# Moving x operands into attention's last slots, down's first steps, and an earlier normed split, in a hybrid encoder step

## The chip, the cores and the metric

The kernel runs on one core of a Trainium2 chip. A core has five engines that run their own instruction queues in order: TensorE (PE, matmuls; its weight loads are shown apart as PEld), VectorE (DVE), ScalarE (ACT), GpSimd (POOL) and SyncE (SP, which here only issues DMA transfers). The engines wait for each other through semaphores. The metric is the device time of one execution in microseconds; less is better.

## The reference

One layer of a streaming encoder is applied to 1024 prompt frames and 32 sample frames of width 1024, all in float32:

```python
h = rms_norm(x, g_mix)
z = h @ w_in                       # q | k | v | conv_h | conv_B | conv_C | gate_a | gate_b
a = window_attn(q, k, v, sink) @ w_attn_out
bo = (cb * causal_conv3(cc * ch)) @ w_conv_out
x = x + (sigmoid(ga) * a + sigmoid(gb) * bo) @ w_mix_out
x = x + mem_attn(rms_norm(x, g_cross) @ w_cq) @ w_co
x = x + square(relu(rms_norm(x, g_mlp) @ w_up)) @ w_down
y = rms_norm(x, g_final)
```

Attention is banded (window 128, chunks of 64 frames, 16 query heads on 4 key heads, a sink in the denominator). K, V, conv states and the memory's keys and values are outputs too.

## The kernel before

**Tiles.** Frames lie along the free dimension in three chunks: 0 and 1 with 384 columns, 2 with 288 (256 prompt and 32 sample frames). The width 1024 lies in 8 blocks f of 128 partitions. Every float32 product is made of three matmuls: an operand is split into a rounded part hi (ACT, L120) and a rest lo (DVE, L121), and `gemm` adds hi·hi, hi·lo and lo·hi (L176 to L178). So each weight tile of 512 KB is loaded by SP (`wr`), split into `wh` and `wl`, and used for 24 matmuls per chunk. `fetch_w`, `issue_w` and `next_w` keep weights up to LOOK = 2 ahead.

**Products in pairs.** For most of the input projection, for up and for down, the chunks 0 and 1 are handled by a scheme of 2x2 block products with fewer multiplications. It needs sums of operands and of weights. For the input projection the operands are, for k = 0 to 3, T2, N1, N3 and N4, made by `x_kind(k)` from the raw inputs: four loads (L801), two multiplications by the norm gain on ACT (L803, L804), one subtraction and three fused multiply-subtracts on DVE (L806 to L810), four hi casts on ACT (L817) and four lo subtractions on DVE and POOL (L819, L821). N4 goes to buffers of the old X1 operands. The weights of a pair come by `pair_fetch` (L829, L830); `pair_issue(key, 4)` first adds them on POOL (L839 to L842) into single buffers s31 and s24 and then splits the sum. `product` runs 12 matmuls (L857 to L859). `x_start` runs the first products of pairs 0 and 1 early; `x_p1` copies a first product out of its bank on ACT (L900) before `x_p2` adds to the same bank. `x_pair` does the rest of a pair; its callbacks ("B11", "W1", "W4", "W3", "W2") fetch and split the next pair's weights.

**Attention's slots.** Attention runs beside the input projection. `hosts` lists 16 column tiles, each with three chunks, so there are 48 slots. For each key head, units of scores, turn (transposes) and values are put at slots by `at`; the fourth head's last unit has its values at slot 45. `sum_step` and `sum_done` add weights of down on POOL in the same slots. At slot 46 `s_begin` calls `open_s`, which closes attention's pool and the kv pool, opens the pools for the pairs in their place, and calls `x_kind(0)` and `x_kind(1)`. The last single column tile, ("b", 1), runs its chunks in the order 1, 0, 2 and carries `x_kind(2)`, `x_kind(3)` and the first pair weights as extras.

**Mix and cross-attention.** `trunk(c)` is a list of 8 items `do_conv_out` and 8 items `do_mix` of chunk c. `beside` puts the steps of cross-attention of the chunk before (`cross_steps`) and late extras between these items. `do_mix` adds to x on DVE (L1101). `do_co` (L1240 to L1242) is cross-attention's output projection; it reads what `Cross.values` split (L1221 to L1227) and its sums are added by DVE (L1245). `normed(c, at)` puts `normed_split(c, f)` behind item at + f: a DVE multiply (L1268), a store, an ACT cast (L1271) and a DVE subtract (L1272), the two DVE operations pinned to program order. It is called with 6 for chunk 0, beside `trunk(2)`.

**Down.** `open_down` opens new pools; PSUM gets six banks `acc` and two `pt`. `steps` is the list (0,0), (0,1), (1,0), (1,1), ... of (j, t): column group j, half t of the hidden blocks k (t = 0: k = 0 to 7, t = 1: k = 8 to 15). `beside_two` runs for each step 24 matmuls of `prod` (chunks 0 and 1) and 24 of `two` (chunk 2), both by `part` (L1654 to L1656), and loads and splits coming operands by `pump`. For the first kind, b11, the blocks k = 0 to 7 lie in Y buffers and 8 to 15 in M buffers; the hidden blocks of chunk 2 lie in Y and H buffers.

**The order of the work.** The program is written down in full and a planner then orders each engine's instructions by dependencies, by program order as priority and by its own simulation of time; instructions given to `pin` keep their order on their engine. A pool opened with `reuse_waits="tile"` lets a new tile wait only for those old tiles whose memory it covers.

Of the kernel before, what the change touches and what calls it, by code (L numbers as in the profile page):

```python
# [38 lines left out]
def hybrid_step(ctx: ExitStack, tc: tile.TileContext, io):  # L39
# [377 lines left out]
    def open_att():  # L417
        closed(st_cm)
        A["cm"], A["pool"] = opened("att", bufs=1, reuse_waits="tile", side="right")
        C["pool"], C["bufs"] = A["pool"], 1  # L420
        C["cvt"] = A["pool"].tile([P, 4, 4], F32, name="cvt")
        W["pool"] = A["pool"]
        do_KS(0)
        do_KS_rest(0)
# [291 lines left out]
    def at(slot, fn):  # L716
        events.setdefault(slot, []).append(fn)
# [30 lines left out]
    for kv, starts in enumerate([(0, 1, 2, 4, 5, 6, 8, 9, 10)] * 3 + [(0, 1, 2, 3, 4, 5, 6, 7, 8)]):  # L748
# [11 lines left out]
        for k in ((5, 8, 11), (2, 5, 8, 11), (2, 5, 8, 11), (2, 5))[kv]:  # L760
            at(base + k, sum_step)
    at(44, sum_done)
    at(46, lambda: s_begin())
    for i, h in enumerate(h for stage in hosts for h in stage):
# [14 lines left out]
    def open_s():  # L779
        closed(A["cm"])  # L780
        closed(kv_cm)
        S["tk_cm"], S["tk"] = opened("tk", bufs=1, reuse_waits="tile")
        S["pw_cm"], S["pw"] = opened("pw", bufs=1, reuse_waits="tile")
        S["cv_cm"], C["pool"] = opened("cv", bufs=1, reuse_waits="tile", side="right")
        C["bufs"] = 2
        C["cvt"] = C["pool"].tile([P, 4, 4], F32, name="cvt")
        S["xk_cm"], S["xk"] = opened("xk", bufs=1, reuse_waits="tile", side="right")
        PW["pool"] = S["pw"]

    PW = {}  # L790
# [5 lines left out]

    def x_kind(k):

        b12, b22, b11, b21 = (S["xk"].tile([P, 384], F32, tag="xk", bufs=8, name=nm("xk")) for _ in range(4))
        for t, c, f in ((b12, 1, k), (b22, 1, k + 4), (b11, 0, k), (b21, 0, k + 4)):  # L800
            sp.dma_start(t, io[f"x{c}"][:, f])  # L801
        g, g4 = col(G_MIX + k), col(G_MIX + k + 4)
        act.mul(b12, b12, g)  # L803
        act.mul(b22, b22, g4)  # L804
        n3 = b22
        dve.tensor_sub(n3, b12, b22)  # L806
        n1, t2, n4 = b12, b11, b21
        dve.scalar_tensor_tensor(n1, b11, g, b12, op0=ALU.mult, op1=ALU.subtract)
        dve.scalar_tensor_tensor(t2, b11, g, n3, op0=ALU.mult, op1=ALU.subtract)
        dve.scalar_tensor_tensor(n4, b21, g4, t2, op0=ALU.mult, op1=ALU.subtract)  # L810
        for kind, x in (("T2", t2), ("N1", n1), ("N3", n3), ("N4", n4)):
            if kind == "N4":
                hi, lo = slot(xpool, "X1", 384), slot(xpool, "X1", 384)
            else:
                hi, lo = (S["tk"].tile([P, 384], F32R, tag="tk", bufs=24, name=nm("tk")) for _ in range(2))
            xk[kind, k] = hi, lo
            act.copy(hi, x)  # L817
            if kind in ("T2", "N1"):
                dve.tensor_sub(lo, x, hi.bitcast(F32))  # L819
            else:  # L820
                pool_e.tensor_tensor(lo, x, hi.bitcast(F32), op=ALU.subtract)  # L821


    raws, wset = {}, {}
# [8 lines left out]
    def pair_issue(key, which):  # L833
        r1, r2 = raws[key][:2]
        a, b = slice(0, 512), slice(512, 1024)
        if which == 4:
            s31 = PW["pool"].tile([P, 1024], F32, tag="s31", name=nm("s31"))
            s24 = PW["pool"].tile([P, 1024], F32, tag="s24", name=nm("s24"))
            pool_e.tensor_tensor(s31[:, b], r2[:, a], r2[:, b], op=ALU.add)  # L839
            pool_e.tensor_tensor(s24[:, a], r1[:, a], s31[:, b], op=ALU.add)  # L840
            pool_e.tensor_tensor(s24[:, b], r1[:, b], s24[:, a], op=ALU.add)
            pool_e.tensor_tensor(s31[:, a], r1[:, a], r2[:, a], op=ALU.add)  # L842
            raws[key] += [s31, s24]
        src = {1: 0, 2: 1, 3: 2, 4: 3}[which]
# [4 lines left out]
        split(hi, lo, raws[key][src])  # L849
        wset[key, which] = (hi, lo)  # L850

    def product(acc, w, half, acts, start):
# [128 lines left out]

    def s_begin():
        open_s()
        for k in range(2):
            x_kind(k)

    ex = [(1, lambda: x_kind(2)), (0, lambda: [x_kind(3), x_fetch(0), x_issue(0, 1), x_fetch(1)]),
          (2, lambda: [x_issue(0, 2), x_issue(1, 1)])]
# [450 lines left out]
    def open_down():  # L1439
# [5 lines left out]
        n_acc = 6  # L1445
        ps.tile([P, 384], F32, tag="pt", bufs=2, name=nm("pt"))

# [98 lines left out]
    normed = lambda c, at: [(at + f, lambda f=f: normed_split(c, f)) for f in range(NF)]  # L1546
    left = beside(left + cross_steps(1), trunk(2), normed(0, 6))
    left = beside(left + cross_steps(2), up0(0) + up0(1), [(min(f + 1, NF - 1), x) for f, x in normed(1, 0)])
# [179 lines left out]

    def beside_two(w, kind, then, half, f, begin, more=(), each=None):

# [14 lines left out]
    def alone(w, kind, then, begin=True, end=True, more=None):  # L1745
        for j, t in steps:
# [6 lines left out]
            if more and (j, t) == (1, 0):  # L1753
# [3 lines left out]
    beside_two(0, "b11", ((*C12, True, False), (*C21, False, False), (*C22, False, False), (*C11, True, False)), 0, 0, True,  # L1757
               twos(1, 0), lambda n: n > 3 and refold(n - 4))
    want(twos(1, 1), ops("n4")[4:], ops("n4")[:4])
# [130 lines left out]
```

## Time and profile before

| what | us |
|---|---|
| three runs | 1788.21, 1789.87, 1792.88 |
| median | 1789.87 |
| the profiled execution, its own time | 1794.17 |
| its span, first to last instruction | 1792.4 |
| PE busy | 1743.3 (97%) |
| DVE busy | 1217.7 (68%) |
| ACT busy | 846.9 (47%) |
| POOL busy | 714.6 (40%) |

The span is what the profiler's rows cover; 1.8 us of the execution lie around it. A row of windows gives a stretch, its length, then for each engine its busy time and the number of instructions, then the granted clock of PE (1.00 is full), the busy share of the DMA engines and their rate. A row of waits names who waited, for which instruction, and the total, the number and the longest of these waits. A row of the timeline gives start, duration, engine, line, operation, output and inputs, and in brackets the idle time before and what ended it.

### The profile page before, as it was taken

Reading aid. Unit: us, or ns where it says so; the run is one execution under the profiler, and the core shown is the slowest. Engines: PE = TensorE matmul, PEld = TensorE weight load, DVE = VectorE, ACT = ScalarE, POOL = GpSimd, SP = SyncE. Lnnn points to the kernel's source line nnn. Section 1 sums busy time; section 2 is a strip of 40 time slices with the busy share of each in tenths; the row PEclk is TensorE's granted clock in tenths of the full one; section 3 lists DMA queues with packets and bytes.
Section 4 is the critical chain, followed back from the end, with each engine's and each line's share of the span. In section 5 each row is a group of like instructions: output and inputs, shape, how many; then the busy total and the mean of one; then the engine's idle time right before and its main releaser. Section 6 shows DMA issues by size and latency. Waiting matters only on the chain.

```text
span 1792.4 us, 30083 instructions
## 1 busy us (share of the span) xinstructions
PE 1743.3 (97%) x11006; PEld 1717.7 (96%) x11006; DVE 1217.7 (68%) x2096; ACT 846.9 (47%) x1624; POOL 714.6 (40%) x749
## 2 busy tenths in 40 slices
PE   8999999999999999999999989999999999999997
PEld 8999999989999999999999989999999989999996
DVE  6768888676787867367666867676665666436673
ACT  8667766842222235144555755632222343324453
POOL 2246676546866654302324242375555200100111
PEclk9999999999999999999999999999999999999998
DMA  5413333342322437779766766744434596545672
GB/s 181 144 60 117 135 127 109 131 155 96 128 97 96 156 120 259 261 256 317 266 201 211 245 215 226 265 152 148 135 131 137 164 307 205 163 132 193 202 249 95
DMA packets 178116, 313.02 MB, mean 175 GB/s; under 512 B 18192, under 2 KB 137776, under 8 KB 177840
## 3 DMA queue, kind: packets, MB, share of 16 engines
q1 hardware_dynamic: 168320, 276.97, 46.6%
q0 software_dynamic: 9216, 33.56, 5.3%
q8 instruction: 86, 1.41, 0.3%
q14 instruction: 62, 0.51, 0.1%
q10 hardware_dynamic: 432, 0.58, 0.1%
HBM read 233.23 MB, written 77.81 MB: 174 GB/s over the span
## 4 chain that ended last, share of the span: by engine, by line
PE 43%; DMA 4%; DVE 2%; issue 2%; ACT 1%; POOL 1%; SPq 0%; POOLq 0%; DVEq 0%; ACTq 0%
PE acc L1655 5%; PE acc L1656 5%; PE acc L1654 5%; PE acc L176 4%; PE acc L177 4%; PE acc L178 4%; PE acc L857 3%; PE acc L859 3%; PE acc L858 3%; PE pa L177 1%; PE pa L176 1%; PE pa L178 1%; DVE wl L121 1%; DMA ct<-m_d 1%; DMA ct<-b_d 1%
## 5 line engine op out<-in xcount | busy, mean ns | idle before, releaser
L121 DVE TENSOR_TENSOR wl<-wr,wh 128x1024 fp32r<-128x1024 f32 (+1 forms) x224 | 321.8, 1437 | 109.0 <-ACT wh L120 107.7
L120 ACT CAST wh<-wr 128x1024 fp32r<-128x1024 f32 (+1 forms) x224 | 234.1, 1046 | 308.4 <-PE acc L1655 76.1
L253 POOL TENSOR_TENSOR xacc<-xacc,ct 128x384 f32<-128x384 f32 (+1 forms) x62 | 75.2, 1214 | 329.2 <-ACT ct L251 326.7
L176 PE MATMUL acc<-Y,wh 128*128 128x384 f32 (+1 forms) x624 | 201.9, 324 | 1.3 <-DVE ct L1296 0.9
L178 PE MATMUL acc<-Y,wl 128*128 128x384 f32 (+1 forms) x624 | 201.9, 324 | 0.9 <-DVE wl L121 0.9
L177 PE MATMUL acc<-Y,wh 128*128 128x384 f32 (+1 forms) x624 | 201.6, 324 | 0.0
L176 PE MATMUL acc<-X,wh 128*128 128x384 f32 (+1 forms) x528 | 172.3, 326 | 0.8 <-ACT wh L120 0.8
L177 PE MATMUL acc<-X,wh 128*128 128x384 f32 (+1 forms) x528 | 171.0, 324 | 1.1 <-DVE X L257 1.1
L178 PE MATMUL acc<-X,wl 128*128 128x384 f32 (+1 forms) x528 | 170.9, 324 | 0.0
L176 PEld LDWEIGHTS acc<-Y,wh 128*128 128x128 f32 x624 | 117.0, 188 | 2.3 <-DVE ct L1296 1.1
L178 PEld LDWEIGHTS acc<-Y,wl 128*128 128x128 f32 x624 | 117.1, 188 | 1.7 <-DVE wl L121 1.7
L177 PEld LDWEIGHTS acc<-Y,wh 128*128 128x128 f32 x624 | 117.1, 188 | 0.0
L570 POOL TENSOR_SCALAR S<-S,rec 128x256 f32<-128x256 f32 (+1 forms) x96 | 91.7, 968 | 59.2 <-DVE rec L567 55.2
L1654 PE MATMUL acc<-Y,wh 128*128 128x384 f32 (+1 forms) x352 | 113.8, 323 | 1.5 <-DVE lt L1408 0.7
L1655 PE MATMUL acc<-Y,wh 128*128 128x384 f32 (+1 forms) x352 | 113.9, 324 | 0.2 <-DVE Y L121 0.2
L1656 PE MATMUL acc<-Y,wl 128*128 128x384 f32 (+1 forms) x352 | 113.6, 323 | 0.0
L120 ACT CAST wh<-s 128x1024 fp32r<-128x1024 f32 x54 | 56.4, 1050 | 107.9 <-PE acc L858 64.1
L177 PEld LDWEIGHTS acc<-X,wh 128*128 128x128 f32 x528 | 99.9, 189 | 2.8 <-DVE X L257 1.9
L176 PEld LDWEIGHTS acc<-X,wh 128*128 128x128 f32 x528 | 99.7, 189 | 2.0 <-ACT wh L120 1.0
L178 PEld LDWEIGHTS acc<-X,wl 128*128 128x128 f32 x528 | 99.8, 189 | 0.8 <-DVE wl L121 0.2
L121 DVE TENSOR_TENSOR Y<-ct,Y 128x384 fp32r<-128x384 f32 (+1 forms) x128 | 69.7, 574 | 29.8 <-ACT Y L120 29.6
L120 ACT CAST Y<-ct 128x384 fp32r<-128x384 f32 (+1 forms) x128 | 59.6, 486 | 58.7 <-DMA ct<-bc_d 14.6
(360 smaller groups left out, 5419.5 us busy)
## 6 DMA issues: line engine op xcount, KB each, us to landing
wr<-in_w_in SPq DMA_DIRECT2D x55, 512.0 KB, 3.3
wr<-in_w_up SPq DMA_DIRECT2D x48, 512.0 KB, 4.1
wr<-in_w_down SPq DMA_DIRECT2D x32, 512.0 KB, 3.7
wr<-wsum_d SPq DMA_DIRECT2D x32, 512.0 KB, 3.9
wl<-wl_d SPq DMA_DIRECT2D x28, 512.0 KB, 5.0
wr<-in_w_conv_out SPq DMA_DIRECT2D x24, 512.0 KB, 4.9
wr<-in_w_mix SPq DMA_DIRECT2D x24, 512.0 KB, 4.5
xacc<-in_w_down POOLq DMA_DIRECT2D x21, 512.0 KB, 4.1
```

The costliest lines, as they stand in the source:

```text
L120: act.copy(hi, src)
L121: dve.tensor_sub(lo, src, hi.bitcast(F32))
L176: pe.matmul(out, wh[:, a], hi, start=(k == 0), stop=False)
L177: pe.matmul(out, wh[:, a], lo, start=False, stop=False)
L178: pe.matmul(out, wl[:, a], hi, start=False, stop=(k == len(acts) - 1))
L253: pool_e.tensor_tensor(acc, acc, sq, op=ALU.add)
L570: pool_e.tensor_scalar_mul(stl[:, h, :nk], stl[:, h, :nk], rec[:, h : h + 1])
L857: pe.matmul(acc, wh[:, a], hi, start=(start and k == 0), stop=False, skip_group_check=True)
L858: pe.matmul(acc, wh[:, a], lo, start=False, stop=False, skip_group_check=True)
L1654: pe.matmul(a, wh[:, s], hi, start=(start and k == 0), stop=False, skip_group_check=True)
L1655: pe.matmul(a, wh[:, s], lo, start=False, stop=False, skip_group_check=True)
L1656: pe.matmul(a, wl[:, s], hi, start=False, stop=(stop and k == len(acts) - 1), skip_group_check=True)
```

## The change

There are three edits.

1. `x_kind` is cut into `x_raw` (loads), `x_sums` (gain and differences) and `x_split` (hi and lo). For k = 0 and 1 loads and sums run at slots 38 to 44, in attention's own buffers: the second KS buffers for k = 0, the conv buffer u and the bias buffer for k = 1. To lay these out, `open_att` names attention's tiles in a chosen order, and `open_s` does so for the pair buffers. `s_begin` closes the kv pool first and splits k = 0 and 1, then fetches pair 0's weights, then loads k = 2 and 3. `pair_sums` is taken out of `pair_issue` and called for pair 0 in the first extras of ("b", 1). The splits of N4 for k = 2 and 3 come last.
2. `normed(0, 6)` becomes `normed(0, 2)`.
3. `open_down` no longer makes a `pt` tile first, and down's first `beside_two` runs its steps as (0,0), (1,0), (0,1), (1,1), and then as before.

```diff
         A["cm"], A["pool"] = opened("att", bufs=1, reuse_waits="tile", side="right")
         C["pool"], C["bufs"] = A["pool"], 1
+        W["pool"] = A["pool"]
+        for i in range(2):
+            for part in "hl":
+                at_tile([P, 4 * P], F32R, f"PT{part}{i}")
+        at_tile([P, 2, P], F32, "AO", 2)
+        at_tile([64, 4, P], F32, "tO")
+        at_tile([P, 4, 257], F32, "S", 2)
+        at_tile([P, 1060], F32, "u")
+        at_tile([P, 4, 256], F32, "ws")
+        at_tile([P, 4, 256], F32, "bias")
         C["cvt"] = A["pool"].tile([P, 4, 4], F32, name="cvt")
-        W["pool"] = A["pool"]
...
     at(44, sum_done)
+    at(38, lambda: x_raw(0))
+    at(40, lambda: x_sums(0))
+    at(42, lambda: x_raw(1))
+    at(44, lambda: x_sums(1))
     at(46, lambda: s_begin())
...
     def open_s():
         closed(A["cm"])
-        closed(kv_cm)
-        S["tk_cm"], S["tk"] = opened("tk", bufs=1, reuse_waits="tile")
...
         PW["pool"] = S["pw"]
+        lt()
+        PW["pool"].tile([P, 384], F32, tag="s1", bufs=2, name=nm("s1"))
+        for tag in ("wl2", "wh2"):
+            PW["pool"].tile([P, 1024], F32R, tag=tag, name=nm(tag))
...
-    def x_kind(k):
-
-        b12, b22, b11, b21 = (S["xk"].tile([P, 384], F32, tag="xk", bufs=8, name=nm("xk")) for _ in range(4))
+    xr = {}
+
+    def x_raw(k):
+        if k == 0:
+            two = [at_tile([P, NT], F32R, t, 2).bitcast(F32) for t in ("KSh", "KSl")]
+        elif k == 1:
+            two = [C["pool"].tile([P, 1060], F32, tag="u", name=nm("u")), at_tile([P, 4, 256], F32, "bias").rearrange("p h k -> p (h k)")]
+        else:
+            two = [S["xk"].tile([P, 768], F32, tag="xk", bufs=4, name=nm("xk")) for _ in range(2)]
+        xr[k] = b12, b22, b11, b21 = [t[:, a : a + 384] for t in two for a in (0, 384)]
         for t, c, f in ((b12, 1, k), (b22, 1, k + 4), (b11, 0, k), (b21, 0, k + 4)):
             sp.dma_start(t, io[f"x{c}"][:, f])
+
+    def x_sums(k):
+        b12, b22, b11, b21 = xr.pop(k)
         g, g4 = col(G_MIX + k), col(G_MIX + k + 4)
...
-        for kind, x in (("T2", t2), ("N1", n1), ("N3", n3), ("N4", n4)):
+        xr["T2", k], xr["N1", k], xr["N3", k], xr["N4", k] = t2, n1, n3, n4
+
+    def x_split(k, *kinds):
+        for kind in kinds:
+            x = xr.pop((kind, k))
...
     def pair_issue(key, which):
...
+        if which == 4 and len(raws[key]) == 2:
+            pair_sums(key)
...
     def s_begin():
+        closed(kv_cm)
+        S["tk_cm"], S["tk"] = opened("tk", bufs=1, reuse_waits="tile")
+        for k in range(2):
+            x_split(k, "T2", "N1", "N3", "N4")
         open_s()
-        for k in range(2):
-            x_kind(k)
-
-    ex = [(1, lambda: x_kind(2)), (0, lambda: [x_kind(3), x_fetch(0), x_issue(0, 1), x_fetch(1)]),
+        x_fetch(0)
+        x_raw(2)
+        x_raw(3)
+        x_sums(2)
+        x_split(2, "T2", "N1", "N3")
+
+    ex = [(1, lambda: [pair_sums(("x", 0)), x_sums(3), x_split(3, "T2", "N1", "N3")]),
+          (0, lambda: [x_split(2, "N4"), x_split(3, "N4"), x_issue(0, 1), x_fetch(1)]),
           (2, lambda: [x_issue(0, 2), x_issue(1, 1)])]
...
         n_acc = 6
-        ps.tile([P, 384], F32, tag="pt", bufs=2, name=nm("pt"))
...
-    left = beside(left + cross_steps(1), trunk(2), normed(0, 6))
+    left = beside(left + cross_steps(1), trunk(2), normed(0, 2))
...
-    def beside_two(w, kind, then, half, f, begin, more=(), each=None):
+    def beside_two(w, kind, then, half, f, begin, more=(), each=None, steps=steps):
...
-               twos(1, 0), lambda n: n > 3 and refold(n - 4))
+               twos(1, 0), lambda n: n > 3 and refold(n - 4), [(0, 0), (1, 0), (0, 1), (1, 1)] + steps[4:])
```

`pair_sums` holds the four additions that stood in `pair_issue`, unchanged.

More of the change, by code (lines that the diff above doesn't have):

```diff
@@ L833, in pair_issue @@
     def pair_issue(key, which):
[L834 to L843, printed above, removed]
+        if which == 4 and len(raws[key]) == 2:
+            pair_sums(key)
         src = {1: 0, 2: 1, 3: 2, 4: 3}[which]
@@ L850, in pair_issue, with pair_sums @@
         wset[key, which] = (hi, lo)
+    def pair_sums(key):
+        r1, r2 = raws[key]
+        a, b = slice(0, 512), slice(512, 1024)
+        s31 = PW["pool"].tile([P, 1024], F32, tag="s31", name=nm("s31"))
+        s24 = PW["pool"].tile([P, 1024], F32, tag="s24", name=nm("s24"))
+        pool_e.tensor_tensor(s31[:, b], r2[:, a], r2[:, b], op=ALU.add)
+        pool_e.tensor_tensor(s24[:, a], r1[:, a], s31[:, b], op=ALU.add)
+        pool_e.tensor_tensor(s24[:, b], r1[:, b], s24[:, a], op=ALU.add)
+        pool_e.tensor_tensor(s31[:, a], r1[:, a], r2[:, a], op=ALU.add)
+        raws[key] += [s31, s24]
     def product(acc, w, half, acts, start):
```

## The prediction

> **What bounds the kernel now.** I read the page first, then the list of waits of TensorE (PE), then windows around the waits, then the timelines of the engines that PE waited for.
>
> ```profile
> span 1792.4 us, 30083 instructions
> ```
> ```profile
> PE 1743.3 (97%) x11006; PEld 1717.7 (96%) x11006; DVE 1217.7 (68%) x2096; ACT 846.9 (47%) x1624; POOL 714.6 (40%) x749
> ```
>
> PE is busy in 97% of the span, so the change can win no more than PE's idle 49.1 us (1792.4 − 1743.3) and what a lowered clock costs. The waits of PE (total, times, longest), asked for 388 to 412, for 1028 to 1042, and for the one that opens down, say where that is:
>
> ```profile
> PE acc L857 <- ACT s L900: 4.2, 1, 4.2
> PE acc L857 <- ACT wh L120: 2.7, 1, 2.7
> ```
> ```profile
> PE acc L1240 <- DVE Gb L1101: 2.3, 2, 1.4
> PE acc L1240 <- ACT Y L1221: 1.7, 1, 1.7
> ```
> ```profile
> PE acc L1654 <- DVE lt L1408: 0.7, 1, 0.7
> ```
>
> Three places stand out, and the three edits lie at them: the start of the x pairs (L857), the output projection of cross-attention beside mix (L1240), the start of down (L1654). Windows at each (length, then busy time and count of PE, PEld, DVE, ACT, POOL, granted clock, DMA share, GB/s):
>
> ```profile
> 330.00:357.00 27.00, 27.00 (x175) 26.20 (x174) 16.36 (x44) 25.88 (x49) 16.17 (x23) 1.00 0.37 130
> 357.00:367.00 10.00, 10.00 (x65) 9.78 (x65) 5.58 (x13) 3.72 (x8) 0.38 (x4) 1.00 0.22 72
> 388.36:392.52 4.16, 0.00 (x0) 0.00 (x0) 4.06 (x7) 2.89 (x7) 1.40 (x2) 0.97 1.01 378
> 392.52:396.32 3.80, 3.80 (x14) 3.80 (x15) 3.61 (x5) 2.99 (x5) 1.70 (x2) 0.58 0.18 65
> 405.74:408.48 2.74, 0.00 (x0) 0.00 (x0) 0.58 (x2) 1.09 (x2) 1.61 (x2) 1.00 0.10 15
> 408.48:412.63 4.15, 4.15 (x15) 4.15 (x16) 3.27 (x4) 1.18 (x2) 1.27 (x1) 0.60 0.33 120
> ```
> ```profile
> 975.00:1004.00 29.00, 28.25 (x201) 27.85 (x199) 15.96 (x33) 16.81 (x36) 4.79 (x5) 1.00 0.72 238
> 1004.00:1028.00 24.00, 24.00 (x184) 23.85 (x183) 23.90 (x45) 19.23 (x42) 7.60 (x7) 1.00 0.68 238
> 1028.00:1042.00 14.00, 9.91 (x44) 8.22 (x44) 11.62 (x21) 7.53 (x14) 8.75 (x7) 0.76 0.81 258
> 1037.23:1042.01 4.78, 4.64 (x17) 4.14 (x18) 3.56 (x6) 2.73 (x6) 1.30 (x3) 0.63 0.59 179
> ```
> ```profile
> 1428.30:1436.46 8.16, 7.49 (x48) 7.52 (x49) 7.03 (x13) 3.55 (x7) 1.17 (x1) 1.00 0.90 273
> 1436.46:1450.40 13.94, 10.71 (x51) 7.66 (x50) 9.59 (x20) 8.65 (x18) 1.01 (x1) 1.00 0.98 326
> 1450.40:1456.20 5.80, 5.80 (x27) 5.80 (x26) 4.66 (x10) 2.00 (x4) 0.00 (x0) 0.71 1.02 354
> ```
>
> Each place has idle PE and, behind it, a stretch in which PE is busy at a clock near half. A stretch of length t at mean clock c loses t × (1 − c): 1.60 us (3.80 × 0.42) and 1.66 us (4.15 × 0.40) at the x pairs, 1.77 us (4.78 × 0.37) at mix, 1.68 us (5.80 × 0.29) at down. So a wait that goes takes its clock loss along.
>
> The Trainium skill, "TensorE: Matmul & The Clock Gate", Part 1, says that the clock halves after an idle window of about 3.4 us, and that gaps up to about 3 us are safe. The trace agrees for the 4.16 us wait; the 2.74 us wait, and the broken waits at mix and down, none longer than 1.7 us, lowered the clock too, so the measurement decides. If the rule alone held, three of the four losses would have another cause and stay (a rival below).
>
> **Part A: x operands loaded and summed in attention.** Before, x_kind begins when attention's buffers are closed:
>
> ```profile
> 366.60 0.37 SPq L600 DMA_DIRECT2D ao_d<-AO  x1
> 367.08 3.73 SPq L801 DMA_DIRECT2D xk<-in_x  x8
> ```
> ```profile
> L803 ACT ACTIVATE xk<-xk,prm x4: 615/616/619, 369.8 to 387.7; 128x384 f32<-128x384 f32 x4
> ```
> ```profile
> 387.72 0.61 ACT L803 ACTIVATE xk<-xk,prm 128x384 f32<-128x384 f32 x1 [0.31 <-DMA xk<-in_x]
> 389.08 0.61 ACT L804 ACTIVATE xk<-xk,prm 128x384 f32<-128x384 f32 x1 [0.74 <-DMA xk<-in_x]
> ...
> 392.00 0.47 ACT L900 COPY s<-acc 128x384 f32<-128x384 f32 x1
> ...
> 392.79 1.98 ACT L120 CAST wh<-s 128x1024 fp32r<-128x1024 f32 x2
> ...
> 407.39 1.99 ACT L120 CAST wh<-s 128x1024 fp32r<-128x1024 f32 x2 [8.93 <-POOL s L841]
> ```
>
> Eight loads go out behind the last attention store. The other eight come late: the first multiply runs at 369.8, the last groups' only at 387.7 to 389.1. ACT takes its queue in order, so the copy L900 that PE needs before it may go on in the same bank stands behind k=3's work until 392.00: the first wait. The casts of pair 0's summed weights come next, at 392.79. Pair 1's sums need the same two single buffers and end only before 407.39: the second wait. Both hang on the late k=2 and k=3.
>
> After the change k=0 and k=1 are loaded and summed in slots 38 to 44, so what stands at the old place is k=2 and k=3, where k=0 and k=1 stood, 17.9 us earlier (387.7 − 369.8). One thing is put ahead of them on SP, pair 0's two weights:
>
> ```profile
> wr<-in_w_in SPq DMA_DIRECT2D x55, 512.0 KB, 3.3
> ```
>
> At 3.3 us to landing each that is up to 6.6 us, so 11.3 us are left. PE's own work up to the wait does not change, so L900 has nothing late ahead of it. Pair 0's four weight sums are called earlier too, ahead of k=3's splits on POOL, and pair 1's follow; they need to gain 2.74 us out of the 11.3. I take both waits as gone: 4.16 + 2.74 + 1.60 + 1.66 = 10.2 us.
>
> What it adds elsewhere goes by the durations (min/median/max in ns) of L803 above and of:
>
> ```profile
> L808 DVE SCALAR_TENSOR_TENSOR xk<-xk,prm,xk x4: 610/993/1519, 372.3 to 393.3; 128x384 f32<-128x384 f32 x4
> ```
> ```profile
> DMA to landing us min/median/max: 2.3/3.5/5.0
> ```
>
> Four ACT multiplies (4 × 0.616 = 2.5 us) and eight DVE operations (4.9 us at 0.61, 12.2 us at 1.52) go into 330 to 357, and eight loads into SP's queue, past the stores of attention and gates. There ACT is busy 25.88 of 27.00 us, so 1.1 us fit and 1.4 us are late; behind it, 357 to 367, ACT idles 6.3 us and takes them up. DVE has 10.6 us free. What queues behind an x multiply that waits for its load is the softmax's exponentials, then the turns and values that PE needs; the DMA share of 0.37 speaks against late loads. No wait of PE lies between 300 and 375. Bounds: 0 (all covered) to 2.5 + 5.0 (no cover, and one longest landing) = 7.5 us; I take 0.5, nearest the row of 6.3 us idle. Below nothing is excluded, because PE has no wait there to lose. Part A: −9.7 us, between −2.7 and −10.2.
>
> A rule speaks against it: the Trainium skill, "SBUF — State Buffer", section "Who interferes with whom", says that a DVE instruction with two SBUF inputs and a GpSimd one that reads SBUF lock each other out for a whole instruction. The spread of L808 from 0.61 to 1.52 us agrees. By it the eight sums cost the 12.2 us end, 1.6 us more than DVE's idle time, and Part A would be −8.1 (a rival below).
>
> The earlier-named tiles and the pools opened in another order only say which old buffer a new one waits for; 0, bounded by the 4.16 us wait coming back.
>
> **Part B: normed_split from item 2 instead of 6.** Per item: two DVE operations, a cast, a store on SP.
>
> ```profile
> L1272 DVE TENSOR_TENSOR Y<-ct,Y 128x384 fp32r<-128x384 f32 x7 | 4.3, 613 | 0.0
> L1268 DVE SCALAR_TENSOR_TENSOR ct<-Gb,prm,R 128x384 f32<-128x384 f32 x5 | 3.8, 768 | 0.0
> ```
>
> Four items move up: 4 × (0.61 + 0.77) = 5.5 us of DVE time leave the stretch where DVE is busy 23.90 of 24.00 us, for 975 to 1004, where it idles 13.0 us and ACT 12.2. The waits on L1101 (2.3 us) are pure DVE backlog and go. The wait on L1221 (1.7 us) is half backlog, half this, which stands ahead of it on ACT:
>
> ```profile
> 1035.60 1.04 ACT L150 CAST wh<-wr 128x1024 fp32r<-128x1024 f32 x1 [1.71 <-DMA wr<-in_w_co]
> ```
>
> That load is paced by buffers, so I leave 0.8 us. With 1.77 us of clock: 2.3 + 0.9 + 1.77 = 5.0; less 0.3 us for the moved casts near softmax work: −4.7 us. Bounds: 0 (the planner lets another item take the room) to −5.8 (2.3 + 1.7 + 1.77).
>
> **Part C: down's first steps, and its banks.** The old second step needs the operands k=8 to 15, which are just arriving:
>
> ```profile
> L121 DVE TENSOR_TENSOR M<-ct,M x8: 541/559/559, 1434.2 to 1441.7; 128x384 fp32r<-128x384 f32 x8
> ```
> ```profile
> L1654 PE MATMUL acc<-M,wh x8: 333/340/443, 1436.5 to 1442.3; 128*128 128x384 f32 x8
> ```
> ```profile
> L121 DVE TENSOR_TENSOR H<-ct,H x11: 449/459/558, 1442.7 to 1450.2; 128x288 fp32r<-128x288 f32 x8, 128x384 fp32r<-128x384 f32 x3
> ```
>
> A step is 48 matmuls, 7.49 us in the first window. With (1, 0) put between, M is first needed near 1436 + 7.5 = 1443.5, behind its last split (1441.7 + 0.6), and H from 1448, with all but the last ones ready. That clears 3.23 us (13.94 − 10.71) and 1.68 us of clock. The pt tile that is no longer made first gives the first sum a bank freed long before, instead of one that DVE empties at L1408: 0.74 us. I leave 0.5 us for the last H tiles, since DMA is at 0.90 to 1.02 throughout. −5.1 us, between −0.7 (the queue of loads only moves the wait on; the bank is left) and −5.7.
>
> **Sum.** −9.7 − 4.7 − 5.1 = −19.5 us. The profiled execution took 1794.17 us (span 1792.4, 1.8 around it), so it would take 1774.7. It lies 4.3 us above the median of the runs, 1789.87; from that, 1770.4 us.
>
> **Rivals.**
> 1. The second x wait stays, because pair 1's sums still queue for the single s31 and s24 buffers. For: L841 ended an idle 8.93 us of ACT. Against: the 11.3 us. A gains 5.3 only (4.16 + 1.60 − 0.5): −15.1, 1774.8. Chance 0.13.
> 2. Mix gains nothing, since ACT's wait for w_co becomes the last: −14.8, 1775.1. Chance 0.12.
> 3. Down's wait comes back a step later, DMA being the bound: C −0.7, so −15.1, 1774.8. Chance 0.10.
> 4. The clock losses of 1.66, 1.77 and 1.68 us (5.1) are not of the short waits and stay: −14.4, 1775.5. That each loss follows a wait speaks against it. Chance 0.05. The page "TensorE: Matmul & The Clock Gate" of the Trainium skill, taken strictly, is this case.
> 5. Nothing moves: the planner orders instructions by its own simulation and may have hoisted or held the same work already: about 1789.9. Against: the 366.60/367.08 rows show a buffer wait that no planner can pass. Chance 0.06.
> 6. Slower: loads held by bias and KS buffers reach the full ACT queue late, and each of the four multiplies waits a longest landing: 4 × 5.0 + 2.5 + 1.6 (DVE over its idle time) = 24.1 us that PE feels, 4.6 more than the 19.5 won: 1794.5 beside 1789.87. It decides once the sums arrive over 19.5 us too late in all. Chance 0.05.
>
> 7. Each of the eight sums on DVE meets an instruction of POOL, as L808's longest did: 12.2 − 10.6 = 1.6 us more, −17.9, 1772.0. POOL's 16.17 us of 27.00 speak against all eight. Chance 0.05. The page "SBUF — State Buffer" of the Trainium skill gives this by its lock.
>
> **How the numbers follow.** The forecast has 0.44. Under 0.3% (5.4 us) is about what a measurement of this kernel cannot tell from no change. Faster: 0.44 + 0.13 + 0.12 + 0.10 + 0.05 + 0.05 = 0.89; same 0.06; slower 0.05. Range: the low end is all upper bounds (10.2 + 5.8 + 5.7 = 21.7, 1768.2), the 1.7 us by which the fastest run (1788.21) lies under the median, and one more clock loss of about that size, 1764.5; the high end is A at −2.7, B at 0, C at −0.7: 1786.5, drawn in to 1784, since all three at their worst is less than 1 in 10.
>
> **What would show it.** Right: x multiplies of k=0 and 1 near 335 to 355; no wait of PE on L900 or wh between 375 and 415 and clock 1.00 there; DVE with idle time between 1004 and 1030; M's first matmul about 7 us behind its last split. Wrong: PE waiting on turns or values between 330 and 370; wh from POOL sums still last at pair 1; PE waiting for H or for weights after 1445.

## The result, and the profile after

The changed kernel takes 1775.5 us (median of 4 runs, 1774.73 to 1777.34), and the kernel before, measured beside it, 1791.38 us (1788.21 to 1793.52). That is 15.9 us less by the medians. The ratio, taken from runs side by side, is 0.9918, with a 95% interval from 0.9899 to 0.9936: 14.7 us, between 11 and 18. Forecast were 1770.4 us, 19.5 less, and a range of 1764.5 to 1784.

The page of the profiled execution of the changed kernel (1774.73 us):

```profile
span 1773.0 us, 30065 instructions
PE 1735.2 (98%) x11006; PEld 1710.7 (96%) x11006; DVE 1216.2 (69%) x2096; ACT 845.2 (48%) x1624; POOL 711.4 (40%) x749
```

PE does the same 11006 matmuls in 8.1 us less busy time, because fewer of them ran at a low clock, and its idle time falls from 49.1 to 37.8 us. Lines have moved: L801 is now L823, L857 is L888, L900 is L931, L1240 is L1279, L1245 is L1284, and L1654 to L1656 are L1692 to L1694.

PE's waits after the change (total, times, longest), for 385 to 412, 330 to 365, 990 to 1042 and 1440 to 1490:

```profile
PE acc L890 <- DVE wl L121: 0.9, 1, 0.9
PE acc L888 <- ACT s L931: 0.7, 1, 0.7
PE acc L888 <- DVE lt L961: 0.7, 1, 0.7
```
```profile
PE pt L589 <- DVE PTl L121: 1.0, 2, 0.9
```
```profile
PE acc L1279 <- DVE Ga L1284: 1.0, 1, 1.0
PE acc L176 <- ACT M L120: 0.7, 1, 0.7
PE acc L1279 <- DVE Gb L1284: 0.6, 1, 0.6
PE acc L176 <- ACT wh L150: 0.4, 1, 0.4
...
```
```profile
PE acc L1694 <- DVE wl L121: 1.7, 2, 1.3
```

At the start of the x pairs the waits of 4.2 and 2.7 us are gone and three short ones are left, 2.3 us together. At mix the waits on L1101 and L1221 are gone, and six others stand there, 3.1 us together; before, the waits between 990 and 1042 came to 4.8 us. Two waits are new at places that had none: on the turns in attention (1.0 us) and on a weight's rest `wl` in down (1.7 us). The windows of the changed kernel (columns as before):

```profile
330.00:357.00 27.00, 26.51 (x169) 24.59 (x167) 16.68 (x44) 25.54 (x49) 16.58 (x23) 1.00 0.39 135
388.00:412.00 24.00, 21.78 (x132) 20.91 (x131) 14.98 (x19) 8.62 (x14) 13.25 (x12) 1.00 0.15 51
1004.00:1028.00 24.00, 23.13 (x162) 21.75 (x161) 22.23 (x38) 17.42 (x34) 13.10 (x13) 1.00 0.69 232
1419.00:1450.00 31.00, 31.00 (x201) 30.80 (x200) 22.09 (x44) 16.36 (x32) 2.18 (x2) 1.00 0.95 309
1450.00:1490.00 40.00, 38.13 (x242) 36.91 (x242) 25.57 (x49) 12.75 (x24) 0.00 (x0) 1.00 0.80 260
```

The granted clock is 1.00 in all of them; no half-clock stretch is left between the ramp and the end of the kernel. Down's start runs with no idle time for 31 us, and the idle time appears behind it, from 1450 on.

To see where the time went I laid the starts of the 11006 matmuls of both profiles side by side, by their number, in steps of 250. The first column is the difference between the two profiles. The second is what the runs with a single edit (first experiments below) show there when their edit belongs to **another** place, so it is how one execution differs from the next.

| matmuls | place | before to after, us | without that edit, us |
|---|---|---|---|
| 2000 to 2500 | attention's last slots | +2.1 | 0.0 |
| 2500 to 2750 | start of the x pairs | −8.0 | −0.8 to −1.8 |
| 3500 to 4000 | x pairs | −1.6 | −0.2 to −0.5 (with edit 1 alone −0.1) |
| 6000 to 6500 | mix | −3.1 | −1.1 to −2.4 |
| 8750 to 9000 | down's first steps | −9.0 | −1.0 to −1.4 |
| 9000 to 9500 | the steps behind them | +3.5 | 0.0 |
| 10500 to 11006 | down's end | −2.2 | −1.3 to −1.9 |
| the rest | | −0.9 | |

The sum is −19.2 us. The last column shows that the profiled execution of before took long at most of these places; it was also 2.8 us over the median of its runs. The medians, −15.9 us, are the better measure of the whole, and the single rows are good to 1 or 2 us.

### The profile page after: what moved, and what is told of

It reads as the page before. It is cut to its first block, busy times and chain, and to the rows that moved or that the text cites. A ratio compares the mean times of both kernels' runs of the same rounds, so it can differ in the third digit from the quotient of the medians.

```text
span 1773.0 us, 30065 instructions
## 1 busy us (share of the span) xinstructions
PE 1735.2 (98%) x11006; PEld 1710.7 (96%) x11006; DVE 1216.2 (69%) x2096; ACT 845.2 (48%) x1624; POOL 711.4 (40%) x749
## 4 chain that ended last, share of the span: by engine, by line
PE 69%; DMA 10%; DVE 7%; issue 5%; ACT 4%; POOL 3%; SPq 1%; POOLq 0%; DVEq 0%; ACTq 0%
PE acc L176 7%; PE acc L177 7%; PE acc L178 7%; PE acc L888 7%; PE acc L890 7%; PE acc L889 7%; PE acc L1693 5%; PE acc L1692 5%; PE acc L1694 5%; PE pa L177 2%; PE pa L178 2%; PE pa L176 2%; DVE wl L121 2%; ACT wh L120 1%; DMA ct<-bc_d 1%
## 5 line engine op out<-in xcount | busy, mean ns | idle before, releaser
L1692 PE MATMUL acc<-Y,wh 128*128 128x384 f32 (+1 forms) x352 | 113.2, 322 | 0.0
L1694 PE MATMUL acc<-Y,wl 128*128 128x384 f32 (+1 forms) x352 | 113.0, 321 | 0.0
```

What stands on the lines that cost most here:

```text
L1692: pe.matmul(a, wh[:, s], hi, start=(start and k == 0), stop=False, skip_group_check=True)
L1694: pe.matmul(a, wl[:, s], hi, start=False, stop=(stop and k == len(acts) - 1), skip_group_check=True)
```

## The experiments

Twelve kernels, each timed in turn with the kernel before on the same chip. My theory was the sum of the prediction; the rivals were that another part of the change did the work, and, once the trace showed new waits in attention and in down, that these have other causes than the ones that the trace names.

### The three edits one by one

`e1_x_only` is the kernel before with edit 1, written here against the changed kernel; `e2_normed_only` and `e3_down_only` are the kernel before with edit 2 or edit 3; `e4_order_only` has the new order of steps and keeps the `pt` tile.

```diff
# e1, against the changed kernel
-    left = beside(left + cross_steps(1), trunk(2), normed(0, 2))
+    left = beside(left + cross_steps(1), trunk(2), normed(0, 6))
...
+        ps.tile([P, 384], F32, tag="pt", bufs=2, name=nm("pt"))
...
-               twos(1, 0), lambda n: n > 3 and refold(n - 4), [(0, 0), (1, 0), (0, 1), (1, 1)] + steps[4:])
+               twos(1, 0), lambda n: n > 3 and refold(n - 4))
```

> The kernel before with the first edit alone (x operands in attention's slots, sums of pair 0 called early). Theory: the parts add up and each is what the trace of the changed kernel shows at its place, counted matmul by matmul against before: attention's last slots 2 us longer, the start of the x pairs 8 us shorter, the pairs 1 us shorter, so about 7 us less than before (1784). Rival, as in the prediction: 9.7 us less (1781.5), and what is missing in the whole is lost where the edits meet. The copy of the first product (L931 here) stands at most 1 us before PE in both.

> The kernel before with normed_split begun at item 2 alone. Theory: the two waits on L1101 go and some smaller ones come, 3 us less than before. Rival, as in the prediction: 4.7 us less. Rival of no gain: another item takes the room on DVE, 0.

> The kernel before with the third edit alone (down's first steps in another order, no pt tile made first). Theory: the 5.6 us at down's first steps go, but a new wait of 1 to 2 us with a half clock behind it comes some 45 us later, where DVE waits for a fold load with a weight's split behind it: 4 to 5 us less than before, with the later waits that the trace of before has near its end perhaps gone too (2 us). Rival: the new wait comes only with the other two edits, since they shift the loads; then 7 to 8 us less here.

> The kernel before with down's first steps in the new order, but the pt tile still made first. Theory: the order carries all but the 0.7 us wait for the bank that DVE empties last (L1408 there), which stays in the trace; the time is 0.7 us above that of the third edit alone, at the edge of what five rounds resolve. Rival: the banks matter more than the order, and most of the gain is missing here.

| kernel | median, us (runs) | ratio, 95% interval | less by, us |
|---|---|---|---|
| before | 1791.59 (27) | | |
| e1, x only | 1784.41 (5) | 0.9959 [0.9943, 0.9975] | 7.2 |
| e2, normed only | 1787.16 (11) | 0.9981 [0.9971, 0.9992] | 4.4 |
| e3, down only | 1786.65 (11) | 0.9982 [0.9973, 0.9992] | 4.9 |
| e4, order only | 1788.33 (11) | 0.9981 [0.9969, 0.9993] | 3.3 |

The last column is the difference of the medians. The parts add up to 16.5 us by it, beside 15.9 for the whole, and by the ratios to 7.3 + 3.4 + 3.2 = 13.9 us, beside 14.7: they don't help or hinder each other by more than can be measured. Each part is known only to a few us. Edit 1 brings 7.2, between 4.5 and 10.2 by its interval, so the forecast 9.7 is neither met nor excluded. Edit 2 brings 1.4 to 5.2 us and edit 3 1.4 to 4.8: the forecast 4.7 lies inside, near the edge, and 5.1 just outside. In e4's profile PE's wait of 0.74 us for the bank that DVE empties at L1408 is still there, and in e3's it is gone, so the `pt` tile does what was said of it; the two ratios can't tell 0.7 us apart.

e3 has the new wait in down as well, and larger. PE's waits there, 1415 to 1500:

```profile
PE acc L1655 <- DVE wl L121: 2.4, 2, 2.1
PE acc L1653 <- DVE Ga L1643: 0.8, 1, 0.8
...
```

So it belongs to edit 3. e3 gains 9.0 us in the first steps, and gives 6.6 back in the 500 matmuls behind them; its two profiles alone would credit the edit with 1 to 2.4 us.

### Four more, three of which the planner undid

After the first four, I moved the eight sums of k = 1 two slots later (`e6_sums1_late`), moved all early loads and sums to slot 46 in the same buffers (`e7_x_late`), and wrote the refold's stores right behind its subtractions (`e5_store_early`). `e8_normed0` starts the normed values at item 0.

```diff
# e5
-            if fold:
-                for to, k in (("n3", "b22"), ("n1", "b12"), ("t2", "b11"), ("n4", "b21")):
-                    sp.dma_start(op_d[to][:, step // 2 - 1], fold[k])
...
                 dve.tensor_sub(fold[to], fold[x], fold[y])
+            for to, k in (("n3", "b22"), ("n1", "b12"), ("t2", "b11"), ("n4", "b21")):
+                sp.dma_start(op_d[to][:, step // 2], fold[k])
# e6
-    at(44, lambda: x_sums(1))
+    at(46, lambda: x_sums(1))
# e7
-    at(38, lambda: x_raw(0))
-    at(40, lambda: x_sums(0))
-    at(42, lambda: x_raw(1))
-    at(44, lambda: x_sums(1))
+    at(46, lambda: [x_raw(0), x_raw(1), x_sums(0), x_sums(1)])
# e8
-    left = beside(left + cross_steps(1), trunk(2), normed(0, 2))
+    left = beside(left + cross_steps(1), trunk(2), normed(0, 0))
```

> The changed kernel with the refolded tiles' four stores issued right behind the subtractions, not at the next even step. Theory: in the changed kernel TensorE's new waits on wl at 1468.65 and 1476.63 (0.34 + 1.34 us) come from VectorE standing 4.37 us at 1476.57 in a subtraction whose fold load waits for a store of the step before; with the stores half a step earlier VectorE no longer stands there and down's first half after its first steps (9000th to 9500th matmul) loses most of its +3.5 us: about 1.7 to 3 us less than the changed kernel, near 1773.5. Rival: VectorE simply has too much work in those steps once they follow each other without a gap; then the waits on wl stay at about 1.7 us and the time at 1775.5.

> The changed kernel with the second step's eight VectorE sums two slots later (slot 46 in place of 44). Theory: the wait of TensorE for pt at 356.35 in attention follows from VectorE's 1.42 us wait at 346.83 for the bias load, which the sums of slot 44 bring in; with the sums two slots later the load has landed, and attention's last slots lose about 1 of their +2.1 us; the start of x may give up to 0.7 us of it back: 1774.5 to 1775.5. Rival: it is the eight sums' own time (some 3 us of VectorE) that delays attention's casts; then the wait moves two slots later and keeps its size, 1775.5.

> The changed kernel with both steps' x loads and sums, in the same buffers, only at slot 46, where attention is done. Theory: the early loads are what removes the 4.2 and 2.7 us waits at the start of x; without them a wait of 4 to 8 us and half-clock losses come back there, attention's +2 us goes: 1779 to 1784. Rival: the new order behind attention (splits as a step of their own, tk opened before, pair sums early) does most of it: then at most 2 us come back, 1774 to 1777.

> The changed kernel with mix's chunk-1 values begun at item 0 in place of 2 (the kernel before: 6). Theory: the 2.2 us of waits left around 997 to 1029 come from other engines' work (Ga on VectorE, M on ScalarE), and not from the values: no change within 0.5 us, 1775 to 1776. Rival: the same effect goes on, another 1 us of 4 items' 3.4: 1774.5; or the values' work now delays the trunk's own casts and a new wait of 1 us or more appears before 990: 1776.5 or more.

| kernel | median, us (runs) | ratio, 95% interval |
|---|---|---|
| before | 1789.16 (11) | |
| e5 | 1778.64 (6) | 0.9934 [0.9914, 0.9953] |
| e6 | 1776.51 (6) | 0.9917 [0.9898, 0.9937] |
| e7 | 1779.41 (6) | 0.9935 [0.9916, 0.9954] |
| e8 | 1782.43 (6) | 0.9953 [0.9935, 0.9970] |

e5, e6 and e7 test nothing of what I meant: on each of the five engines their instructions stand in the same order as in the changed kernel. The rows that I should have read before are the issues of x loads, L823 of the changed kernel:

```profile
L823 SPq DMA_DIRECT2D xk<-in_x x8: 380/430/431, 372.6 to 375.9; - x8
...
L823 SPq DMA_DIRECT2D KSh<-in_x x2: 419/436/453, 279.8 to 280.2; - x2
...
L823 SPq DMA_DIRECT2D u<-in_x x2: 346/386/425, 310.5 to 310.9; - x2
L823 SPq DMA_DIRECT2D bias<-in_x x2: 333/382/432, 344.4 to 344.8; - x2
```

The loads into `KSh` go out at 279.8 us, long before slot 38, and those into `u` at 310.5. The planner puts a load where its buffer comes free, so the slot in the source set nothing in these three kernels; the buffer did. The bias buffer is free last, at 344.4, and that load is late.

The three are still useful, as repeats of one program in a second measurement: 18 runs from 1772.58 to 1783.45 us, median 1778.3, which is 10.8 us less than before there. Their ratios, 11.6 to 14.8 us less, overlap the first one, 0.9918 [0.9899, 0.9936]. So the gain is some 11 to 16 us, and a single execution of this kernel lies anywhere within 11 us.

e8 does differ. It is slower than its three neighbours by 3 to 6 us; the intervals overlap, but five of its six runs lie at or above 1781.35 us, and fifteen of those eighteen below. PE's waits between 990 and 1055:

```profile
PE o L1251 <- DVE PTl L121: 2.0, 1, 2.0
PE acc L1279 <- DVE Gb L1284: 1.9, 1, 1.9
PE acc L176 <- ACT M L120: 1.3, 1, 1.3
...
```

PE now waits for the rest of the softmax's transposed weights (`PTl`), which DVE makes at 1014.09. In DVE's queue before it stand four operations of `normed_split` (2.3 us between 1005 and 1011.2), and then the softmax's own scaling, three operations in 1.91 us where the changed kernel took 1.11. That the normed work begun earlier is what makes `PTl` late fits this, but is not shown. My expectation of no change was wrong, and the second half of its rival, a new wait, was right; I put it before 990 us, and it came at 1012.

### What the early loading is worth: the buffers taken away

These two undo edit 1's loading in a way that the planner can't pass: both steps, or only k = 1, are loaded into the pool that opens behind attention, as before. The pools' order, the splits ahead of later loads and the earlier weight sums stay.

```diff
# e10, both_behind (lines of x_raw, then of s_begin; the four at() lines are gone)
-        if k == 0:
-            two = [at_tile([P, NT], F32R, t, 2).bitcast(F32) for t in ("KSh", "KSl")]
-        elif k == 1:
-            two = [C["pool"].tile([P, 1060], F32, tag="u", name=nm("u")), at_tile([P, 4, 256], F32, "bias").rearrange("p h k -> p (h k)")]
-        else:
-            two = [S["xk"].tile([P, 768], F32, tag="xk", bufs=4, name=nm("xk")) for _ in range(2)]
+        two = [S["xk"].tile([P, 768], F32, tag="xk", bufs=4, name=nm("xk")) for _ in range(2)]
...
+        open_s()
         for k in range(2):
+            x_raw(k)
+            x_sums(k)
             x_split(k, "T2", "N1", "N3", "N4")
-        open_s()
# e11, second_behind (k = 1 alone, in s_begin)
-        for k in range(2):
-            x_split(k, "T2", "N1", "N3", "N4")
+        x_split(0, "T2", "N1", "N3", "N4")
         open_s()
+        x_raw(1)
+        x_sums(1)
+        x_split(1, "T2", "N1", "N3", "N4")
```

> The changed kernel with both steps' x operands loaded into the pool that opens behind attention, as in the kernel before, and everything else of the change kept (the pools' order, the splits ahead of the other loads, the pair's sums earlier). The run with only the slots changed had the same schedule, since the planner places the loads where their buffers come free; with these buffers it can't. Theory: the early loads are what removes the waits at the start of x: a wait of 3 to 5 us and half-clock stretches come back there, some 6 to 8 us of the 8.0; attention's order is again that of before and its +2.1 us goes: 1779.5 to 1782. Rival: the order behind attention brings most of the gain: 1774 to 1776.

> The changed kernel with the first step's x operands early as in the change, the second step's behind attention. Theory: VectorE's 1.4 us wait for the load into bias at 346.8 is gone, and with it the wait of 0.85 us at 356.35, so attention costs about 1.1 and not 2.1 us; at the start of x the first wait stays away, and a wait of 1 to 3 us for the second step's operands comes: 1775.5 to 1778. Rival for attention's cost: it is the planner's other order of attention's own matmuls and VectorE work, and not that load: the +2.1 us stays as it is.

Before took 1790.66 us here. e10 took 1790.45 us (11 runs; ratio 0.9996 [0.9986, 1.0007]), e11 1777.04 us (6 runs; 0.9931 [0.9916, 0.9945]). PE's waits in e10 from 385 to 412, and from 495 to 510:

```profile
PE acc L879 <- ACT s L922: 2.8, 1, 2.8
PE acc L880 <- DVE tk L839: 1.9, 3, 1.4
PE acc L879 <- ACT tk L837: 1.5, 1, 1.5
PE acc L879 <- DVE lt L952: 0.7, 1, 0.7
```
```profile
PE acc L879 <- DVE lt L946: 3.7, 1, 3.7
```

and ACT in e10 just before the first of them ends:

```profile
390.53 0.62 ACT L819 ACTIVATE xk<-xk,prm 128x384 f32<-128x384 f32 x1 [0.28 <-DMA xk<-in_x]
391.06 0.49 ACT L837 CAST tk<-xk 128x384 fp32r<-128x384 f32 x1
391.46 0.47 ACT L922 COPY s<-acc 128x384 f32<-128x384 f32 x1
```

That is the picture of the kernel before: the copy that PE needs stands in ACT's queue behind a multiply of a late x operand. The early buffers are what removes it. The time that I expected, 1779.5 to 1782, was still missed by over 8 us. The rival, that the new order behind attention brings most of the gain, is dead: with that order alone the start of x takes as long as before (−0.2 us), and the stretch from the 3000th matmul loses another 4.1 us to the wait of 3.7 us and the lower clock behind it. e10 has edits 2 and 3 too, which brought 9.3 us alone by the medians and 6.6 by the ratios, and still ends level with before. The 4.1 us account for about half of the first figure and most of the second; where the rest went I could not place.

e11 says that with k = 0 alone in early buffers the whole can't be told apart from the changed kernel: the ratios overlap, and the time is within the 1775.5 to 1778 expected. The start of x gains 5.1 us in its profile and not 8.0, and attention costs 0.4 us and not 2.1.

**Attention's cost.** DVE in the changed kernel, in the last slots:

```profile
346.83 0.62 DVE L833 SCALAR_TENSOR_TENSOR u<-bias,prm,u 128x384 f32<-128x384 f32 x1 [1.42 <-DMA bias<-in_x]
```

DVE stands 1.42 us in a sum of k = 1 for the load into bias, and attention's own work queues behind it. In e11 that wait is gone, and so is PE's wait on L589. But the link is weak: all eight profiles with the early k = 1, the one above among them, have this DVE wait (1.4 to 1.8 us), and PE's waits on L589 in them run from 1.0 us in all down to none, the cost of the stretch from 2.1 to 0.4 us. The late load is one condition for that cost; whether it reaches PE changes from run to run. The second order of attention's own matmuls, which the planner chose in all of these, e11 too, costs no more than 0.4 us.

### What gives back part of down's gain

The view of DVE in down, changed kernel:

```profile
1476.57 0.56 DVE L1528 TENSOR_TENSOR fold<-fold,fold 128x384 f32<-128x384 f32 x1 [4.37 <-DMA fold<-b_d]
1477.04 1.22 DVE L121 TENSOR_TENSOR wl<-wr,wh 128x1024 fp32r<-128x1024 f32 x1
```

`refold` takes four operand tiles per block from memory, subtracts them and stores them. Its subtraction (L1528) waits 4.37 us for its load, and the weight's split, for which PE waits 1.3 us, is next in DVE's queue. From 1430 to 1500 DVE waits 12.8 us for these loads. Two edits were to break this chain:

```diff
# e9, fold_pool
-                dve.tensor_sub(fold[to], fold[x], fold[y])
+                pool_e.tensor_tensor(fold[to], fold[x], fold[y], op=ALU.subtract)
# e12, fold_queue
-                    sp.dma_start(op_d[to][:, step // 2 - 1], fold[k])
+                    pool_e.dma_start(op_d[to][:, step // 2 - 1], fold[k])
-                    sp.dma_start(fold[k], op_d[k][:, step // 2])
+                    pool_e.dma_start(fold[k], op_d[k][:, step // 2])
```

> The changed kernel with the refold's sixteen subtractions on POOL in place of VectorE. Theory: TensorE's new waits for wl in down (1.7 us in the changed kernel, 2.9 us with the stores written earlier, where the planner kept the order) come from VectorE standing 4.4 us in a refold subtraction whose load is late, with the weight's split queued behind it; without that queue the waits on wl around 1468 and 1477 us go, and the 9000th to 9500th matmul lose 1.5 to 3 of the +3.5 us: 1773 to 1774. Rival: the weight itself arrives too late there, or POOL's subtractions slow VectorE down; the waits keep their size and the time stays at 1775.5 or rises by 1 us.

> The changed kernel with the refold's sixteen loads and sixteen stores issued on POOL's queue in place of SP's; the subtractions stay on VectorE. Theory: in down's first half the refold's transfers stand in SP's queue between the weights and the operands (with the subtractions on POOL, SP waited 12.4 us there and the second half's operands came 4.5 us later), and with steps that follow each other without a gap this queue is what is late; off it, the loads go out when their tile is free, VectorE's 4.4 us wait shrinks, and the 9000th to 9500th matmul lose 2 to 3.5 of the +3.5 us of the changed kernel: 1772 to 1773.5, with TensorE's waits on wl and Y around 1468 to 1486 us gone. Rival: the DMA engines themselves, 82% busy from 1440 to 1500 us, set when these loads land; the waits on wl keep about 1.7 us in all and the time stays within 1 us of 1775.5.

e9 took 1780.17 us (5 runs; 0.9940 [0.9926, 0.9954]), e12 1779.26 us (6 runs; 0.9945 [0.9928, 0.9962], before 1790.25). Neither is faster than the changed kernel, and both of the times expected, 1773 to 1774 and 1772 to 1773.5, were missed by some 6 us. PE's waits in e9 from 1440 to 1495, and SP's largest there:

```profile
PE acc L1692 <- ACT Y L120: 2.5, 1, 2.5
```
```profile
SPq L1521 <- POOL fold L1528: 12.4, 14, 3.8
```

With the subtractions off DVE, the waits on `wl` are gone, so DVE's queue did cause those. But POOL's subtractions are slower (1.07 us each in the median, beside 0.56 on DVE), SP stands 12.4 us waiting to store them, the loads of the second half's operands go out behind that, and PE waits 2.5 us for one of them: the matmuls from 9000 to 9500 cost 4.7 us, which is no better than the 3.5 to 5.1 us that e5, e6, e7 and the changed kernel, all one program, cost there. So I took SP's queue for the culprit, and e12 does not bear that out. PE's waits in e12 from 1430 to 1500, DVE's, the share of the refold's transfers from 1440 to 1490 (now alone on their own queue, q0), and the landing times of its loads:

```profile
PE acc L1693 <- DVE H L121: 2.1, 2, 1.4
PE acc L1694 <- DVE wl L121: 1.0, 1, 1.0
...
```
```profile
DVE fold L1528 <- DMA fold<-b_d: 10.9, 4, 5.8
```
```profile
q1 hardware_dynamic: 7023, 7.78, 50.6%
q0 software_dynamic: 1792, 5.51, 31.6%
```
```profile
DMA to landing us min/median/max: 2.6/5.6/7.2
```

The refold no longer stands in SP's queue, and its loads land later, 5.6 us in the median beside 4.5 in the changed kernel. DVE waits 10.9 us for them, little less than the 12.8 before; PE waits 3.8 us beside 1.7, now for operands H as well, and the matmuls from 8750 to 9500 cost 3.5 us more than in the changed kernel's profile, and about 2 us more than in those of e5 and e7. The wait for the loads is still there, as the rival had it: the refold's 5.5 of 13.4 MB share DMA engines that are busy 0.88 of 1419 to 1450 and 0.79 of 1450 to 1490 (0.95 and 0.80 in the changed kernel) with the operands and weights of the same steps. Two changes of queue and engine moved the wait and none removed it.

That the DMA engines are the last word is argued, not shown, and the traces hold another cause that no run tests: the four `fold` buffers. A load into one goes out only when the store from it has landed. SP in the changed kernel, from 1430 to 1500, and POOL in e12, before these loads (L1525):

```profile
SPq L1525 <- DMA t_d<-fold: 4.3, 2, 2.6
```
```profile
POOL fold L1525 <- DMA n_d<-fold: 10.9, 6, 4.4
```

Load, subtraction, store and the next load form a chain through four buffers, whatever the queue. A kernel with more `fold` buffers, one with the refold's transfers left out, or one with them some steps later would tell; none was run.

## Why the prediction was right, and where its sizes were off

**Part A, forecast −9.7, measured −7.2 alone.** The mechanism held: both waits and both clock losses went, and e10 shows that the early buffers did it. Two terms were mis-sized. "I take both waits as gone: 4.16 + 2.74 + 1.60 + 1.66 = 10.2 us" left nothing in their place, and 2.3 us of short waits stayed (8.0 us in the profile, of which 1 to 2 are the long execution of before). "I take 0.5" for attention was too little in most runs (0.4 to 2.1). It missed that DVE, with 10.6 us free, can still be late when it stands in order behind one load, and I looked for that on ACT. "PE waiting on turns or values between 330 and 370", one of the signs of being wrong, came, for 1.0 us; so did a wait on the copy (L931) between 375 and 415, for 0.7 us. The slot numbers misled me about the time: I put the x multiplies of k = 0 and 1 near 335 to 355 us, and they run at 283.5 and 313.1. The estimate for k = 2 and 3, up to 6.6 us behind the old 367.08, was near: the loads go out from 372.6.

**Part B, forecast −4.7, measured −4.4 alone.** DVE's backlog went: 24.0 us of 1004 to 1028 are now busy for 22.23. The rival that ACT's wait for w_co takes its place fell; 0.4 us on L150 is left. What was not seen is how close the optimum lies: two items further, in e8, costs 3 to 6 us. The sum also left out the waits that came in place of the old ones, 3.1 us in the changed kernel. Mix gains 3.1 us in the profile, and 1.1 to 2.4 us without the edit, so the profile alone would credit it with 1 to 2 us; −4.4 is the figure of the runs, with the interval above, and its size agrees with the forecast partly by luck.

**Part C, forecast −5.1, measured −4.9 alone (−3.2 by the ratio).** The first steps gained more than I counted (9.0 us, of which 1.0 to 1.4 are the long execution of before), and "the queue of loads only moves the wait on", which I gave as the bound, happened in part: 9.0 us won, 3.5 given back in the same profile. I asked for it under "what would show it wrong", PE waiting for weights after 1445, and so it did, for 1.7 us. The nearly right sum came out of two terms that were both too small, which is luck. The sign "M's first matmul about 7 us behind its last split" did not follow from the working, where the two lie 1.2 us apart (1443.5 and 1442.3); in the trace they lie 0.6 us apart, and PE does not wait.

**The sum.** −19.5 us was the difference of the two profiled executions nearly to the tenth (−19.4), but for a wrong reason: they differ by some 5 us at places that no edit touches. All the priced waits were read from one execution, which took 1 to 2 us more than others at each of the three places. By medians the gain is 15.9 us in the first measurement and 10.8 in the repeats, and 19.5 lies above the interval of either.

**The rivals.** The second wait did not stay; loads did not block attention for more than 2.1 us; the eight sums on DVE took 5.6 us together, near the 4.9 of the low bound and far from the 12.2 of the lock: these are dead. "Down's wait comes back a step later" came true in part, as said. The half-clock losses went with the waits, so the rival taken from the Trainium skill, "TensorE: Matmul & The Clock Gate", Part 1 (the clock halves after an idle window of about 3.4 us), fell too: here 1.5 to 1.8 us of idle time in a window were enough, as the last section shows.

## What to carry to other kernels

Where a planner orders the instructions, the buffer that a load goes into can decide when it starts, as here; before moving a line, look in the trace at when the load is issued now. A gap that is closed brings forward all the transfers behind it, so ask which of them share the DMA engines with the next steps, and expect part of the gain back there. And price a wait from more than one execution: here a stretch differed by 1 to 2 us between runs of the same instructions, as much as a whole term of the sum.

## What the runs showed of the clock

Eleven of the fourteen profiles (before, after and the twelve) have stretches at half clock in the middle of the kernel. They last 3.41 us or twice that, and within one profile their starts lie whole multiples of 3.413 us apart: in before the second, third and fourth start 5, 188 and 310 such steps behind the first. So the clock is granted in windows on a grid that stays fixed within a profile. Windows laid on that grid (the second column is the length, the third PE's busy time, the eighth the clock) show what decides. Before, at the second wait:

```profile
405.93:409.34 3.41, 0.86 (x5) 0.86 (x6) 1.28 (x2) 1.95 (x2) 1.42 (x2) 1.00 0.28 80
409.34:412.75 3.41, 3.41 (x12) 3.41 (x11) 2.49 (x5) 0.44 (x2) 1.39 (x1) 0.50 0.21 78
```

e11, at a wait of 1.98 us in mix:

```profile
999.98:1003.39 3.41, 1.43 (x11) 1.21 (x10) 2.27 (x4) 1.64 (x5) 1.21 (x1) 1.00 0.55 177
1003.39:1006.80 3.41, 3.41 (x16) 3.41 (x16) 3.02 (x10) 2.64 (x9) 0.00 (x0) 0.51 0.24 89
```

e10, at its wait of 2.8 us:

```profile
387.43:390.84 3.41, 1.75 (x14) 1.51 (x12) 3.34 (x5) 0.83 (x2) 1.38 (x1) 1.00 0.67 207
390.84:394.26 3.42, 2.28 (x13) 2.29 (x14) 1.95 (x4) 3.42 (x7) 0.00 (x0) 1.00 0.85 271
```

A window in which PE idled 2.55 or 1.98 us (3.41 − 0.86, 3.41 − 1.43) is followed by a window at half clock. The longer wait of 2.8 us lies across a border, 1.66 and 1.14 us on its sides, and costs no clock. Over all the profiles, 22 windows at full clock were followed by half clock: in 21 of them PE idled 1.82 us or more, in one 1.51 (e3, from 1027.67). Nine windows with 1.62 to 1.82 us of idle time escaped, and none with more. In a window that is itself at half clock, 1.07 us was enough to stay there. So the border lies between about 1.5 and 1.8 us; the ends of matmuls are modelled in these profiles, which may be why it is not sharper. Several short waits in one window add up, as they did before the half-clock stretches at mix and down: the windows there idled 2.03 and 1.82 us, with no single wait over 1.7. The price is at most half of 3.41, 1.7 us for each window, as the stretches of before showed. So a wait near 2 us costs between 2 and 3.7 us, depending on where the grid falls in that run.
